# Which pairs of the output projection use seven products, and which use an adding transfer

## The chip, the cores and the metric

The kernel runs on one core of one Trainium2 chip. The metric is the time of one execution on the device, in microseconds; lower is better. A run gives the median of several executions. One more execution is recorded by the hardware profiler, and everything said of single instructions comes from that one.

A core has five engines, each with its own instruction queue, which it works through in order: TensorE (PE; its weight loads are shown as PEld), VectorE (DVE), ScalarE (ACT), GpSimd (POOL) and SyncE (SP). Transfers are started by an engine's queue and carried out by 16 DMA engines that all queues share.

## What is computed

The reference is one layer of a streaming encoder for 256 tokens of 2048 features: a SwiGLU block, a mixer of two recurrent branches, cross-attention over 256 memory tokens, a second SwiGLU block and a norm. Cut to what matters here:

```python
x = x + 0.5 * swiglu(rms_norm(x, ffn1_norm), ffn1_w_up, ffn1_w_down)
h = rms_norm(x, mix_norm)
...
merged = g[:, :, 0, :] * (y_a @ w_branch_a) + g[:, :, 1, :] * (y_b @ w_branch_b)
x = x + merged @ w_out
x = x + cross_attention(rms_norm(x, xattn_norm), rms_norm(mem, mem_norm),
                        xattn_wq, xattn_wkv, xattn_wo)
x = x + 0.5 * swiglu(rms_norm(x, ffn2_norm), ffn2_w_up, ffn2_w_down)
return rms_norm(x, final_norm)
```

The change is in `merged @ w_out`, a product of 256x2048 by 2048x2048. It is called the output projection here.

## The kernel before

**Pieces.** All weights come from memory in pieces of 128 partitions by 2048 float32, 1 MB each, in one planned order for the whole kernel (`plan`). `weights` takes the next piece and keeps up to two prepared ahead of the product that uses them. There are three `raw` buffers for what a transfer brings, three `h` and three `l` buffers for what is made of it.

**High and low halves.** TensorE multiplies in a format with a shortened mantissa. So each operand is split into a high half (ScalarE copies it into the short format, `h`) and a low half (VectorE subtracts, `l = raw - h`; `split`, lines 153 and 154). A product of two operands is three matmuls: high by high and low by high (line 698), high by low (line 700). In `three`, all matmuls of line 698 of a piece come first, then those of line 700, so the low halves of the weights are wanted last.

**Adding transfers.** For some pieces the low half isn't made by VectorE. `begin_added` loads the piece, ScalarE writes `l = -high` (line 289), and a transfer started by GpSimd adds the piece to it on the way in (line 290). That costs a second transfer of the same megabyte, and it is begun one piece earlier in the plan than the piece itself, holding a raw and an l buffer from then on. The high half is then copied at the piece's own turn (line 298).

**The output projection.** Its 2048 output columns are done in two groups of 1024. Each group takes eight pieces, one for each pair of K tiles (2 x 128 rows of `w_out`), so a pair is 256 rows by 1024 columns. With 256 tokens that is a product of 2x2 blocks by 2x2 blocks (token tile by K tile, K tile by half of the columns). A pair is of one of two kinds, set by a letter in `PAIRED`:

- mixed (`m`, or `M` with an adding transfer): eight block products, 24 matmuls of 128x512. Its low half is one VectorE operation of 2048 columns (`m`) or the adding transfer (`M`).
- fast (`f`): seven block products after Strassen's scheme in Winograd's form, 21 matmuls. It needs sums and differences of the weights' blocks (`td`, lines 334, 336 and 338 on VectorE), and these have to be split as well (`th`, `tl`).

Both kinds add into the same seven banks of PSUM (numbers 0 to 6 in `PRODUCTS`). Banks 0, 4 and 5 are used by fast pairs alone. So when the last fast pair of a group is done, `add_residual` with `final` false adds those three to the residual x (one ScalarE copy and six VectorE operations, lines 681 to 685). Behind the last pair of the group, with `final` true, it adds the other four (line 688).

The other operand, the merged activations, is prepared by `Pairs.add` in a turn: eight transposes on TensorE (line 550) and copies and splits on ScalarE and VectorE, for two pairs at a time. For a fast pair it makes four sums (line 630) and splits 512 columns, for a mixed one a difference (line 639) and 256 columns.

**What comes before and after.** The branch projection (`w_branch_a`, `w_branch_b`, lines 393, 394 and 399) precedes; its 16 pieces make the merged activations. After it comes the Q projection of the attention (lines 367 and 370), whose operand is the normed x. That operand, too, is made in turns, `normed`: transposes of x (line 550), scaled copies on ScalarE (line 446), low halves on VectorE (line 448). Each turn makes two of the 16 operands. The first half of x is complete after group 0. Its four turns are held in the list `late`, and `behind_out` lets one of them go behind chosen pairs of group 1. The Q projection begins with products over operands 0 to 7, the ones of these four turns.

**Two other streams** share the queues here. `make_ahead` forms sums of the last block's weights ahead of time: a load into `prep`, four VectorE operations (line 227) and a store (line 228), the load and the store in GpSimd's queue. SP's queue carries all loads of pieces, in plan order. Within an engine the order is laid down when the program is built, mostly that of the text, but an instruction whose operands are expected later can be put behind others that are ready.

Of the kernel before, what the change touches and what calls it, by code (L numbers as in the profile page):

```python
# [46 lines left out]
KINDS = {"m": "mixed", "M": "mixed", "f": "fast", "a": "fast"}  # L47


PAIRED = {"out": "m0 f1 M2 f3 m4 f5 M6 m7"}  # L50


def kinds(name):
    return [e[0] for e in PAIRED[name].split()]

# [38 lines left out]
def block_kernel(ctx: ExitStack, tc: tile.TileContext, xT, xin, memT, vec, gfin, bgate, lruw, wu1, wd1, win, wv,  # L94
# [306 lines left out]
    def flush(late, n=KT):  # L401
        while late and n:
            late.pop(0)()
            n -= 1
# [897 lines left out]
    xs3, sq3 = Operands(), TokenSquares()  # L1302

    def behind_out(g, p):
        if not g or p in (1, 3, 5, 6):
            flush(late, 1)

    for g in range(2):
        pair_products("out", g, pairs_m, add_residual, behind_out)
        for c in (2 * g, 2 * g + 1):  # L1310
            if c == 2:
                root_ready(xt[c])
            sq3.add(c)
            late += [lambda c=c, y=y: normed(xs3, c, "xattn_norm", [y]) for y in range(2)]
# [265 lines left out]
```

## Time and profile before

| what | value |
|---|---|
| median of 3 runs | 2405.73 us (2405.52 to 2405.76) |
| the profiled execution's own time | 2406.76 us |
| its span, first to last instruction | 2405.0 us |
| TensorE clock granted | 0.999 |
| busy: PE, DVE, ACT, POOL | 100%, 85%, 65%, 5% of the span |
| DMA | 640.03 MB, mean 266 GB/s |
| output projection, first to last matmul | 1429.9 to 1515.9 us |
| transfers of `w_out` | 16 loads, 4 adding transfers |

The profile lists busy times by engine, groups of instructions by line, what an idle engine waited for, and the chain of work that ended last, followed back from the end. `acc<-h,ops` means that an instruction writes the tile `acc` and reads `h` and `ops`. In a timeline a row has the start, the duration, the engine, the line and the operation; `xN` are N instructions merged into one row, and a bracket at the end gives the idle time before it and what ended that. Matmuls overlap in the pipeline, so the time that one costs in a row of many is the distance between starts and not its duration.

### The profile page before, as it was taken

What the parts mean: (1) busy time and instruction counts of PE and PEld (TensorE: products, weight loads), DVE (VectorE), ACT (ScalarE), POOL (GpSimd) and SP (SyncE); (2) the same over time, 40 slices, a digit from 0 to 9 for tenths busy, and PEclk for the clock granted to TensorE, in tenths of its full rate; (3) what the DMA queues carried; (4) which work ended last, traced back from release to release, by engine and by line L of the source; (5) the groups of instructions that cost most, each with busy time, mean ns of one, the idle gap of its engine ahead of it and who ended that gap; (6) DMA issues with size and microseconds to landing.
All of it is one profiled execution on the core that took longest, in us unless ns stands there. A gap on an engine that the chain in (4) does not pass through costs nothing.

```text
span 2405.0 us, 31008 instructions
## 1 busy us (share of the span) xinstructions
PE 2393.3 (100%) x12053; PEld 1991.5 (83%) x12053; DVE 2054.2 (85%) x2335; ACT 1560.6 (65%) x1594; POOL 120.1 (5%) x174
## 2 busy tenths in 40 slices
PE   9999999999999999999999999999999999999998
PEld 7888888888888888888888888888888888888887
DVE  7679999999999866778678788765799999999995
ACT  6756777777777654454576456655676677777774
POOL 0000000000000000000000000000000000000000
PEclk9999999999999999999999999999999999999999
DMA  8876889999999757767678768764687899999993
GB/s 301 309 254 223 268 266 266 273 274 278 276 276 276 266 216 291 265 243 289 258 276 334 281 243 262 294 223 162 215 321 299 317 276 276 274 274 273 274 272 129
DMA packets 98739, 640.03 MB, mean 266 GB/s; under 512 B 10976, under 2 KB 11488, under 8 KB 32928
## 3 DMA queue, kind: packets, MB, share of 16 engines
q1 hardware_dynamic: 74160, 493.61, 54.8%
q0 software_dynamic: 24288, 144.19, 24.5%
q8 instruction: 94, 1.54, 0.2%
q14 instruction: 53, 0.43, 0.0%
q10 hardware_dynamic: 144, 0.26, 0.0%
HBM read 601.18 MB, written 36.83 MB: 265 GB/s over the span
## 4 chain that ended last, share of the span: by engine, by line
PE 97%; DVE 2%; DMA 1%; ACT 0%; issue 0%; SPq 0%; ACTq 0%; DVEq 0%
PE acc L698 38%; PE acc L700 19%; PE acc L367 11%; PE acc L393 7%; PE acc L394 7%; PE acc L399 7%; PE acc L370 6%; PE acc L738 1%; PE acc L550 1%; DVE tl L154 1%; DVE l L154 0%; PE acc L1342 0%; PE acc L1088 0%; DMA raw<-t 0%; PE acc L1367 0%
## 5 line engine op out<-in xcount | busy, mean ns | idle before, releaser
L153 ACT ACTIVATE h<-raw 128x2048 fp32r<-128x2048 f32 (+3 forms) x420 | 683.2, 1640 | 412.6 <-PE acc L394 135.0
L154 DVE TENSOR_TENSOR l<-raw,h 128x2048 fp32r<-128x2048 f32 (+2 forms) x365 | 751.6, 2060 | 227.4 <-ACT h L153 224.9
L698 PE MATMUL acc<-h,xh 128*128 128x512 f32 x1221 | 474.6, 391 | 0.6 <-ACT h L153 0.5
L698 PE MATMUL acc<-h,xl 128*128 128x512 f32 x1221 | 473.1, 390 | 0.0
L153 ACT ACTIVATE h<-td 128x1024 fp32r<-128x1024 f32 x287 | 301.0, 1055 | 172.3 <-DVE td L334 53.7
L154 DVE TENSOR_TENSOR tl<-td,h 128x1024 fp32r<-128x1024 f32 x287 | 348.9, 1220 | 13.7 <-ACT h L153 11.8
L698 PE MATMUL acc<-h,hidop 128*128 128x512 f32 x1408 | 351.4, 391 | 0.0
L698 PEld LDWEIGHTS acc<-h,hidop 128*128 128x128 f32 x1408 | 262.7, 188 | 53.8
L698 PEld LDWEIGHTS acc<-h,xh 128*128 128x128 f32 x1221 | 229.1, 188 | 54.6 <-ACT h L153 5.8
L698 PEld LDWEIGHTS acc<-h,xl 128*128 128x128 f32 x1221 | 229.3, 188 | 46.7
L393 PE MATMUL acc<-h,ops 128*128 128x512 f32 x576 | 226.1, 393 | 0.0
L394 PE MATMUL acc<-h,ops 128*128 128x512 f32 x576 | 224.4, 390 | 0.0
L367 PE MATMUL acc<-ops,h 128*128 128x512 f32 x896 | 217.7, 393 | 0.0
L700 PE MATMUL acc<-tl,xh 128*128 128x512 f32 x660 | 193.0, 394 | 0.3 <-DVE tl L154 0.3
L367 PEld LDWEIGHTS acc<-ops,h 128*128 128x128 f32 x896 | 164.1, 188 | 32.6
L700 PE MATMUL acc<-l,hidop 128*128 128x512 f32 x704 | 190.7, 389 | 0.0
L334 DVE TENSOR_TENSOR td<-raw 128x1024 f32<-128x1024 f32 x146 | 178.0, 1219 | 3.5 <-DMA raw<-wout 2.3
L700 PE MATMUL acc<-l,xh 128*128 128x512 f32 x561 | 156.7, 390 | 0.0
L700 PEld LDWEIGHTS acc<-l,hidop 128*128 128x128 f32 x704 | 132.1, 188 | 27.8
L700 PEld LDWEIGHTS acc<-tl,xh 128*128 128x128 f32 x660 | 120.7, 188 | 33.8 <-DVE tl L154 10.1
L399 PE MATMUL acc<-l,ops 128*128 128x512 f32 x576 | 142.3, 389 | 0.0
L399 PEld LDWEIGHTS acc<-l,ops 128*128 128x128 f32 x576 | 108.1, 188 | 22.4
(270 smaller groups left out, 3014.4 us busy)
## 6 DMA issues: line engine op xcount, KB each, us to landing
raw<-wu SPq DMA_DIRECT2D x151, 1024.0 KB, 6.9
raw<-wd SPq DMA_DIRECT2D x88, 1024.0 KB, 7.3
l<-wu POOLq DMA_DIRECT2D x59, 768.0 KB, 8.7
raw<-win SPq DMA_DIRECT2D x40, 1024.0 KB, 4.9
raw<-wg SPq DMA_DIRECT2D x32, 1024.0 KB, 5.4
prep<-wu POOLq DMA_DIRECT2D x25, 1024.0 KB, 7.1
t<-prep POOLq DMA_DIRECT2D x25, 1024.0 KB, 4.6
raw<-t SPq DMA_DIRECT2D x25, 1024.0 KB, 6.5
```

Of the source, the lines that this page charges most:

```text
L153: done["high"] = act.activation(h, raw, ACT.Copy).ins
L154: done["low"] = dve.tensor_tensor(out=l, in0=raw, in1=h.bitcast(F32), op=ALU.subtract).ins
L334: dve.tensor_tensor(out=two[0], in0=raw[:, None, :512].broadcast_to([P, 2, 512]), in1=two[1], op=ALU.subtract)
L367: pe.matmul(acc, h[:, k * P:(k + 1) * P], xs[k], start=k == 0, stop=False)
L370: done["product"] = pe.matmul(acc[:, :T], l[:, k * P:(k + 1) * P], xs[k][:, :T], start=False, stop=k == KT - 1).ins
L393: pe.matmul(accs[t], x[:, t * P:][:, :P], h[j], start=first and j == 0, stop=False)
L394: pe.matmul(accs[t], x[:, T + t * P:][:, :P], h[j], start=False, stop=False)
L399: done["product"] = pe.matmul(accs[t], x[:, t * P:][:, :P], l[j], start=False, stop=last and j == 3).ins
L550: pe.transpose(acc[:, z * T + t * P:][:, :P], tile[:, t * 512 + (2 * y + z) * P:][:, :P], ident)
L698: pe.matmul(acc, a, b, start=start, stop=False)
L700: done["product"] = pe.matmul(acc, ah, bl, start=False, stop=stop).ins
L738: pe.transpose(acc[:, z * T + t * P:][:, :P], hid[t][:, (2 * y + z) * P:][:, :P], ident)
```

## The change

```diff
-PAIRED = {"out": "m0 f1 M2 f3 m4 f5 M6 m7"}
+PAIRED = {"out": "M0 f1 M2 f3 m4 f5 f6 m7"}
...
     def behind_out(g, p):
-        if not g or p in (1, 3, 5, 6):
+        if not g or p in (1, 3, 6, 7):
             flush(late, 1)
```

In both groups pair 6 becomes a fast pair, so that four of eight pairs use seven products where three did. Pair 0 takes an adding transfer; pair 6, which had one, no longer does. The last fast pair of a group is now pair 6 and not pair 5, so the partial eviction moves behind pair 6. In group 1 the four turns of x go behind pairs 1, 3, 6 and 7 instead of 1, 3, 5 and 6.

## The prediction

> **What bounds the kernel.** I read the page's shares first, then the chain of work that ended last, then the chain in order of time around the output projection, then VectorE's and the queues' timelines there.
>
> ```profile
> span 2405.0 us, 31008 instructions
> PE 2393.3 (100%) x12053; PEld 1991.5 (83%) x12053; DVE 2054.2 (85%) x2335; ACT 1560.6 (65%) x1594; POOL 120.1 (5%) x174
> PE 97%; DVE 2%; DMA 1%; ACT 0%; issue 0%; SPq 0%; ACTq 0%; DVEq 0%
> ```
>
> TensorE is busy the whole span and makes up 97% of the chain. A matmul taken away anywhere shortens the end, unless its successor then waits. VectorE at 85% is the only engine near it. The chain through the stage (start, length, matmuls):
>
> ```profile
> 1430.05 3.63 PE acc L698 x16
> 1433.68 1.82 PE acc L700 x8
> ...
> 1456.96 3.17 PE acc L698 x14
> 1460.14 1.59 PE acc L700 x7
> 1461.72 3.63 PE acc L698 x16
> ...
> 1467.16 3.63 PE acc L698 x16
> ...
> 1510.09 0.44 PE acc L550 x4
> ...
> 1514.20 1.81 PE acc L700 x8
> 1516.02 1.81 PE acc L367 x8
> ```
>
> Each pair is 16+8 matmuls (mixed) or 14+7 (fast), with line 700 taking the low halves of the weights. Pair 6 of group 0 runs from 1461.72 to 1467.16, 5.44 us for 24: one matmul per 0.2267 us. (The mean durations in the page's groups are of overlapping matmuls and would overstate the gain.) Pair 5 (fast) takes 4.76 us for 21. No gap stands between pairs, so the stage is TensorE's alone. How near VectorE is (PE, PEld, DVE, ACT, POOL busy per group of columns):
>
> ```profile
> 1429.90:1472.44 42.54, 42.54 (x192) 35.08 (x191) 38.63 (x43) 26.32 (x23) 2.32 (x3) 1.00 0.88 275
> 1472.44:1515.86 43.42, 43.42 (x201) 35.91 (x200) 36.89 (x41) 30.30 (x34) 3.04 (x5) 1.00 0.86 284
> ```
>
> VectorE is busy for 91% of group 0 and 85% of group 1: this change spends that reserve.
>
> **Pair 6 by seven products.** It removes three matmuls per group: 2 x 3 x 0.2267 = 1.36 us, all on the path. The Trainium skill (TensorE: Matmul & The Clock Gate, "Wait — 56ns, not 53.3ns?") has warm 512-column matmuls start every 215.7 ns, by which this term would be 1.29 us. The rows above have 226.7 ns, and the measurement decides.
>
> Where pair 6 gave VectorE nothing (its low half came by an adding transfer), it now takes what fast pair 5 takes:
>
> ```profile
> 1450.29 1.22 DVE L334 TENSOR_TENSOR td<-raw 128x1024 f32<-128x1024 f32 x1
> ...
> 1452.15 1.75 DVE L154 TENSOR_TENSOR l<-raw,h 128x1536 fp32r<-128x1536 f32 x1
> ...
> 1454.42 2.44 DVE L154 TENSOR_TENSOR tl<-td,h 128x1024 fp32r<-128x1024 f32 x2
> 1456.77 2.86 DVE L227 TENSOR_TENSOR prep<-prep 128x512 f32<-128x512 f32 x4
> 1460.36 2.29 DVE L154 TENSOR_TENSOR l<-raw,h 128x2048 fp32r<-128x2048 f32 x1 [0.72 <-ACT h L153]
> ...
> 1466.79 0.69 DVE L682 TENSOR_TENSOR ev<-acc,ev 128x512 f32<-128x512 f32 x1
> ```
>
> From 1450.29 to 1456.77, 6.48 us in all. Pair 0's plain split (2.29 us, as in the 1460.36 row) goes in exchange. Its operand, too, becomes a fast pair's: in the turn of the last merged columns, behind pair 0 of group 0, four small operations and a split of 512 columns take the place of one and a split of 256.
>
> ```profile
> 1394.49 1.02 DVE L630 TENSOR_TENSOR xs<-xs 128x128 f32<-128x128 f32 x4
> 1397.26 0.69 DVE L154 TENSOR_TENSOR xd<-xs,xd 128x512 fp32r<-128x512 f32 x1 [0.24 <-ACT xd L153]
> 1415.87 0.42 DVE L639 TENSOR_TENSOR xs<-xs 128x256 f32<-128x256 f32 x1
> 1416.77 0.42 DVE L154 TENSOR_TENSOR xd<-xs,xd 128x256 fp32r<-128x256 f32 x1 [0.48 <-ACT xd L153]
> ```
>
> That is 1.71 for 0.84, 0.87 us more, in group 0 alone. Its window then asks VectorE for 38.63 + 6.48 + 0.87 - 2.29 (the next group's pair 0 is split inside it) = 43.7 us against 42.54 - 0.68 = 41.9 us of TensorE. Group 1 asks 36.89 + 6.48 = 43.4 against 42.7. What doesn't fit slips past the window's end, as far as TensorE's slack allows, so order decides. ScalarE is far from this (26.32 of 42.54).
>
> In group 0 pair 5 is followed by line 227 (traced after pair 5's split, so ahead of pair 6's), done by about 1459.6, or up to 0.9 later with the larger operand. Pair 6's preparation then ends 6.48 us later, between 1466.1 and 1467.0. Pair 6 starts at 1461.72 and wants its last low half after 14 + 5 matmuls, at 1466.03. That is 0.1 to 1.0 us late, and less if matmuls of pair 7 are put in between; I take 0.4, since VectorE's idle gaps before that (one of 0.72 us in the 1460.36 row) close.
> ```profile
> 1451.62 1.06 ACT L153 ACTIVATE h<-td 128x1024 fp32r<-128x1024 f32 x1
> ...
> 1503.60 2.29 DVE L154 TENSOR_TENSOR l<-raw,h 128x2048 fp32r<-128x2048 f32 x1 [4.46 <-ACT h L153]
> ```
>
> ScalarE's two splits of the sums (1.06 each) must wait for pair 5's h buffer (three exist), free 14 matmuls into pair 5, at 1460.14; the sums are wanted from matmul 7 of pair 6, at 1463.1: room enough. In group 1 VectorE idles 4.46 us ahead of pair 7's split, so pair 6 fits there.
>
> The partial eviction (six VectorE operations like the 1466.79 row, 4.1 us at most) moves from behind pair 5 to behind pair 6. Its banks are wanted by pair 0 of the next group, one pair later: 5.44 us of pair 7 cover it where 10.88 did. Only the first three of the six free banks: even behind pair 7's split they are through 2.29 + 3 x 0.69 = 4.4 us after pair 6. I take 0; uncovered it would be that 4.4.
>
> **Adding transfers for pairs 0.** Their number stays two per group; pair 0's replaces pair 6's. Pair 0 now takes a raw, an l buffer and a place in SP's and POOL's queues one piece before the last piece of the branch projection.
>
> ```profile
> raw<-wab SPq DMA_DIRECT2D x16, 1024.0 KB, 5.0
> ...
> 1404.50 0.33 SPq L307 DMA_DIRECT2D raw<-wout  x1
> 1411.11 1.92 ACT L153 ACTIVATE h<-raw 128x2048 fp32r<-128x2048 f32 x1 [3.52 <-PE acc L394]
> 1413.06 2.29 DVE L154 TENSOR_TENSOR l<-raw,h 128x2048 fp32r<-128x2048 f32 x1 [1.16 <-ACT h L153]
> 1420.67 2.29 DVE L154 TENSOR_TENSOR l<-raw,h 128x2048 fp32r<-128x2048 f32 x1
> 1426.74 0.53 POOL L228 DMA_DIRECT2D t<-prep  x1 [18.55 <-DVE prep L227]
> 1424.65 1.92 ACT L289 ACTIVATE l<-raw 128x2048 fp32r<-128x2048 f32 x1 [0.27 <-PE acc L399]
> L290 POOL DMA_DIRECT2D l<-wout x4: 856/878/888, 1427.3 to 1491.1; - x4
> ...
> DMA to landing us min/median/max: 9.1/10.1/10.9
> ```
>
> The last projection piece gets pair 0's place in SP's queue (1404.50), lands 5.0 us later and is wanted by ScalarE at 1411.11: covered by 1.6 us, and its product only starts at about 1424.6 (24 x 0.2267 before 1430.05). Its VectorE split leaves 1413.06, since pair 0 took the l buffer, and takes the place that pair 0's own split leaves at 1420.67. Pair 0's transfer (last row: the four of line 290) can be issued at about 1415.0 (it takes the l buffer of the 1413.06 row, then ScalarE's 1.92 of the 1424.65 row), ahead of line 228's store, which waits until 1426.74 anyway; it lands by 1425.9 and is wanted at 1433.68. In group 1: buffer free at 1456.96, landed by 1469.8, wanted at 1475.5 (3.63 into that pair, which starts 4.76 + 5.44 after 1461.72). Cover 7.8 and 5.7 us: 0. Without that cover each would cost what it is late.
>
> **Turns behind other pieces.** In group 1 the four turns of x (lines 550, 446, 448) go behind pairs 1, 3, 6, 7 instead of 1, 3, 5, 6. The last one used to have pair 7's 5.44 us after it. Now line 367's first product of Q follows, and its seventh and eighth matmuls read what this turn makes.
>
> ```profile
> 1509.93 0.60 PE L550 MATMUL acc<-vt,x 128*128 128x128 f32 x4
> 1510.57 0.84 ACT L446 ACTIVATE ops<-acc,vt 128x256 fp32r<-128x256 f32 x2 [0.29 <-PE acc L550]
> 1487.04 0.87 DVE L448 SCALAR_TENSOR_TENSOR ops<-acc,vt,ops 128x256 fp32r<-128x256 f32 x2
> 1513.46 2.28 DVE L154 TENSOR_TENSOR l<-raw,h 128x2048 fp32r<-128x2048 f32 x1
> 1515.66 1.88 DVE L688 TENSOR_TENSOR x<-acc,x 128x512 f32<-128x512 f32 x3
> ```
>
> Pair 7 ends at 1516.02 - 1.36 = 1514.66. The turn's matmuls cost 0.44 us wherever they stand. The Q product starts at 1515.1 and reaches its seventh matmul 6 x 0.2267 later, at 1516.46. ScalarE is done 0.64 + 0.84 after 1514.66, at 1516.1. VectorE is then in the three operations of line 688 (1.88, from pair 7's end) until 1516.5, and hands over the operands at 1516.95 and 1517.4: TensorE waits 0.5 to 0.7 us. Lower end 0, if TensorE's order puts other matmuls of Q in between (the low halves and the second product's first six are ready). Upper end 2.8, if a weight split of 2.28, which here stood just ahead of line 688, stands ahead of the turn too. I take 0.4, near the row of line 688, since those operations become ready first.
>
> **Sum.** -1.36 + 0.4 + 0.4 = -0.56 us. The profiled execution took 2406.76 us (span 2405.0 and 1.76 around it), 1.03 above the median; it would come to 2406.2, and the median 2405.73 to **2405.2**. About 0.2%, 4.8 us, is what a measurement of this kernel can tell from no change; this is 0.02%.
>
> **Rivals.**
> A, the forecast: 2404.6 to 2405.8, chance 0.45.
> B, every wait is filled by other matmuls: -1.36, or up to 0.5 more if the lighter start of group 0 helps: 2403.9 to 2404.6. For: no pair of the stage waits in the chain above. Against: VectorE is asked for more than TensorE. 0.25.
> C, the Q product waits for the turn behind a weight split, 2.8 us: -1.36 + 0.4 + 2.8 = +1.8, 2407.6, slower than before. It decides if line 154 stands between pair 7's end and line 448. For: the 1513.46 row. Against: there it fills idle time of VectorE, which after the move is gone. 0.15, from 2406 on by how much of it other matmuls fill.
> D, VectorE's backlog holds pair 6: if a split (2.2) or line 227 (2.86) is ahead of the preparation's last part, each group waits that long: -1.36 + 4.4 to 5.7, 2408.8 to 2410.1. Bound: if all VectorE idle of both groups (42.54 - 38.63 + 43.42 - 36.89 = 10.4) remains beside 87.1 us of work, the stage takes 97.5 for 86.0, 2417. Against: 4.46 us of that idle lies right where group 1 needs it. 0.12.
> E, pair 0's adding transfer is slow: at twice 10.9 us it lands 3.1 us late in group 0 and 5.2 in group 1, -1.36 + 8.3 = +6.9, 2412.6. Against: four such transfers landed within 9.1 to 10.9 us under a VectorE that was 85 to 91% busy. 0.03. The Trainium skill (SBUF — State Buffer, "SBUF: two separate sides") warns of just this: descriptors of a GpSimd-issued transfer can't be written while VectorE holds the shared port, 620 ns becoming 3100. The same page has tensor_tensor outside the mode that does it, and the four landings agree.
>
> That the change does less than it says is hardly possible: one string sets plan, operands and products alike.
>
> **Numbers.** Range 2404.0 to 2407.5: A, B and most of C; D, E and the ends left out come to about 0.2. Slower by over 0.2%: E and a quarter of D, 0.06. Faster by over 0.2%: nothing gives 4.8 us; 0.01. Same: 0.93.
>
> **What would show it.** 12047 matmuls for 12053; 180 plus turns per group. Stage from 1430.05 to the first line 367 matmul: between 84.6 and 85.7 us for 85.97. Right before pair 6's end, line 154's tl<-td on VectorE ends within 1 us of its reader in group 0. Behind pair 7 of group 1, line 367 pauses after six matmuls, with line 448 as releaser. The forecast is wrong if the stage is longer than 86, or if another stage moves by over 1 us.

## The result and the profile after

The change made the kernel slower: median 2413.3 us (2412.05 to 2415.75, 7 runs) against 2405.73 (7 runs by then, 2404.64 to 2408.42), a ratio of 1.0031 with a 95% interval of 1.0021 to 1.0040. The forecast of 2405.2 and its range, up to 2407.5, are both missed. The profiled execution of the changed kernel took 2412.34 us (span 2410.6), 5.6 more than that of the kernel before.

The page of the kernel after, its span, busy times and shares of the chain:

```profile
span 2410.6 us, 31006 instructions
PE 2394.0 (99%) x12047; PEld 1990.8 (83%) x12047; DVE 2062.5 (86%) x2348; ACT 1563.6 (65%) x1598; POOL 120.4 (5%) x174
PE 95%; DVE 2%; DMA 1%; ACT 1%; issue 1%; SPq 0%; ACTq 0%; DVEq 0%
```

The six matmuls are gone (12047 for 12053), but TensorE is no longer busy throughout. Where it stands idle is read from the windows of the two groups of columns and of the Q projection up to the first attention matmul (line 1342); the columns are length, PE, PEld, DVE, ACT and POOL busy with instruction counts, granted clock, DMA share and GB/s. Kernel after:

```profile
1428.96:1470.70 41.74, 41.74 (x190) 34.54 (x188) 41.74 (x50) 25.06 (x23) 2.04 (x3) 1.00 0.74 218
1470.70:1518.66 47.96, 43.78 (x197) 34.95 (x196) 41.74 (x43) 30.51 (x33) 3.04 (x5) 1.00 0.80 271
1518.66:1545.91 27.25, 25.10 (x147) 21.34 (x146) 19.81 (x32) 19.29 (x33) 0.00 (x0) 1.00 0.71 272
```

The same windows of the kernel before; its first group stands in the prediction (42.54):

```profile
1472.44:1515.86 43.42, 43.42 (x201) 35.91 (x200) 36.89 (x41) 30.30 (x34) 3.04 (x5) 1.00 0.86 284
1515.86:1539.92 24.06, 24.06 (x145) 21.31 (x144) 17.40 (x26) 17.04 (x31) 0.00 (x0) 1.00 0.72 275
```

Group 0 is 0.80 us shorter, a little more than its three matmuls, and TensorE never waits in it. Group 1 is 4.54 us longer, and the Q projection 3.19 us longer. Together that is +6.9 us. (The execution after entered the stage 0.93 us earlier, 1428.96 against 1429.89, so its span shows less.) The two places, in TensorE's timeline of the kernel after; the bracket is the idle time before the row:

```profile
1475.68 0.61 PE L700 MATMUL acc<-l,xd 128*128 128x512 f32 x2
1477.78 1.19 PE L698 MATMUL acc<-h,ops 128*128 128x512 f32 x4 [1.48 <-ACT h L153]
...
1480.10 1.20 PE L698 MATMUL acc<-h,xd 128*128 128x512 f32 x4 [0.66 <-ACT h L153]
...
1482.67 0.73 PE L700 MATMUL acc<-tl,xd 128*128 128x512 f32 x2 [0.69 <-DVE tl L154]
...
1485.44 0.74 PE L698 MATMUL acc<-h,xd 128*128 128x512 f32 x2 [1.35 <-ACT h L153]
...
1492.18 1.07 PE L698 MATMUL acc<-h,ops 128*128 128x512 f32 x4
...
1518.66 2.03 PE L367 MATMUL acc<-ops,h 128*128 128x512 f32 x6
1522.85 0.96 PE L367 MATMUL acc<-ops,h 128*128 128x512 f32 x2 [2.15 <-DVE ops L448]
```

The first place is pair 1 of group 1, with some of pair 2 woven into it: four waits, 4.2 us. Pairs 1 and 2 with a turn should take 4.76 + 5.44 + 0.44 = 10.6 us; they take 16.0, from 1476.14 (the first row and two starts) to 1492.18. (The waits in brackets are counted from the modelled ends of matmuls, so the distances between starts show more.) The second place is the seventh matmul of Q. It should start 6 x 0.2267 after 1518.66, at 1520.0, and starts 2.8 us later.

What the first place waits for is read in the queues, SP's first, of the kernel after:

```profile
1449.57 0.33 SPq L288 DMA_DIRECT2D raw<-wout  x1
1454.75 0.33 SPq L307 DMA_DIRECT2D raw<-wout  x1
1461.10 0.33 SPq L288 DMA_DIRECT2D raw<-wout  x1
1464.20 2.86 SPq L327 DMA_DIRECT2D raw<-wout  x2
...
1458.85 0.89 POOL L290 DMA_DIRECT2D l<-wout  x1 [29.30 <-DVE tl L154]
1463.78 0.56 POOL L228 DMA_DIRECT2D t<-prep  x1 [4.05 <-DVE prep L227]
...
1460.35 0.68 DVE L338 TENSOR_TENSOR td<-raw,td 128x512 f32<-128x512 f32 x1
...
1462.27 1.91 ACT L298 ACTIVATE h<-raw 128x2048 fp32r<-128x2048 f32 x1
...
1476.18 1.23 DVE L334 TENSOR_TENSOR td<-raw 128x1024 f32<-128x1024 f32 x1 [4.07 <-DMA raw<-wout]
```

There are three raw buffers. Pair 0 of group 1 takes one at 1449.57 and gives it back only when its high half is copied (line 298), at 1464.18: 14.6 us. Pair 1's load takes that buffer. Pair 6, now fast, holds another until its last difference is made (line 338, until 1461.03), and pair 2's load, which stands first in the queue, takes that one. So SP begins no load between 1454.75 and 1461.10. Then pair 0's adding transfer (1458.85), pair 2's load (1461.10), the store of line 228 (1463.78) and the loads of pairs 1 and 3 (from 1464.20) come on top of one another. Pair 1's load takes 12.0 us, to 1476.18. Before, it left and landed like this:

```profile
1462.68 4.54 SPq L327 DMA_DIRECT2D raw<-wout  x2
...
1470.99 1.23 DVE L334 TENSOR_TENSOR td<-raw 128x1024 f32<-128x1024 f32 x1 [0.52 <-DMA raw<-wout]
```

8.3 us. Counted from the first matmul of the stage the load now leaves 2.4 us later (35.2 us into it, not 32.8) and is 3.7 us slower on the way. The DMA share tells the same (the column before the last, then GB/s). Before:

```profile
1440.00:1460.00 20.00, 20.00 (x90) 16.48 (x89) 18.93 (x20) 13.89 (x10) 0.89 (x1) 1.00 0.78 240
1460.00:1475.00 15.00, 15.00 (x68) 12.43 (x67) 12.13 (x14) 8.39 (x8) 1.43 (x2) 1.00 0.99 347
```

After:

```profile
1440.00:1460.00 20.00, 20.00 (x90) 16.58 (x89) 20.00 (x22) 13.29 (x13) 0.89 (x1) 1.00 0.55 201
1460.00:1475.00 15.00, 15.00 (x67) 12.40 (x67) 12.11 (x16) 6.62 (x5) 1.19 (x2) 1.00 0.99 301
```

In the 20 us in which the engines have room (0.55), the loads can't start; in the next 15 the engines are full and bring less.

The second place, in the chain of waits of the kernel after, in order of time:

```profile
1508.95 2.30 DVE l L154
1511.27 8.27 DMA raw<-wq
1519.64 1.91 ACT h L153
1521.55 0.74 ACT ops L446 x2
1522.31 0.49 DVE ops L448
1522.85 0.96 PE acc L367 x2
```

The turn's copies (line 446) stand on ScalarE's queue behind the copy of a piece of Q (line 153), which waits for a load that left at 1511.27 and lands at 1519.6. So the Q product waits for a late load, through ScalarE's queue. Nothing of VectorE's stands in front of line 448 itself, but the load could leave only when a split on VectorE (line 154, the first row) gave up its raw buffer.

**Theories.** *Buffers and transfers* (mine, after the result): pair 0's adding transfer in group 1 holds a raw buffer, the loads bunch up, pair 1 and later a piece of Q come late. *VectorE* (rival D of the prediction): the four operations of a fast pair 6 and the sums of line 227 push its splits back. *Turn* (rival C): most of the loss is the turn's new place, whatever the loads do. *Slow adding transfer* (rival E).

### The profile page after: what moved, and what is told of

Same layout as the page of the kernel before. It is cut to its first block, busy times and chain, and to the rows that moved or that the text cites. A ratio compares the mean times of both kernels' runs of the same rounds, so it can differ in the third digit from the quotient of the medians.

```text
span 2410.6 us, 31006 instructions
## 1 busy us (share of the span) xinstructions
PE 2394.0 (99%) x12047; PEld 1990.8 (83%) x12047; DVE 2062.5 (86%) x2348; ACT 1563.6 (65%) x1598; POOL 120.4 (5%) x174
## 4 chain that ended last, share of the span: by engine, by line
PE 95%; DVE 2%; DMA 1%; ACT 1%; issue 1%; SPq 0%; ACTq 0%; DVEq 0%
PE acc L698 36%; PE acc L700 18%; PE acc L367 11%; PE acc L393 7%; PE acc L394 7%; PE acc L399 7%; PE acc L370 6%; PE acc L738 1%; DMA raw<-wout 1%; DVE l L154 1%; PE acc L550 1%; ACT h L153 0%; DVE tl L154 0%; DMA raw<-wq 0%; PE acc L1342 0%
## 5 line engine op out<-in xcount | busy, mean ns | idle before, releaser
L154 DVE TENSOR_TENSOR tl<-td,h 128x1024 fp32r<-128x1024 f32 x291 | 353.5, 1220 | 13.7 <-ACT h L153 11.9
```

Source lines behind the costliest of these rows:

```text
L154: done["low"] = dve.tensor_tensor(out=l, in0=raw, in1=h.bitcast(F32), op=ALU.subtract).ins
```

## The experiments

All are edits of the kernel after unless said. "Stage" is the time from the first matmul of the output projection to the first of Q (85.97 before, 89.70 after), which doesn't depend on when an execution reaches it. Ratios are to the kernel before, timed on the same chip (2405.46 to 2405.73 us).

### The change in parts

**The turns put back, all else kept.**

```diff
-        if not g or p in (1, 3, 6, 7):
+        if not g or p in (1, 3, 5, 6):
```

> The changed kernel with the turns of x behind pairs 1, 3, 5, 6 of group 1, as before the change. In the changed kernel TensorE waits in two places: in pair 1 of group 1 (4.2 us) and at the first Q product (2.2 us, some 3 with what follows). If the turn's new place is the cause of the second wait: that wait is gone, pair 1's stays, and the time is 2.2 to 3.2 us below the changed kernel's, about 2410.5. If the second wait comes from late loads and not from the place: it stays in some form, within 1 us of 2413.3.

2410.12 us, 1.0019 (1.0010 to 1.0028). The stage stays at 89.68 and Q to attention falls from 27.25 to 24.41. The waits of TensorE that are left (total, times, longest) are those of pair 1:

```profile
PE acc L698 <- ACT h L153: 3.3, 3, 1.3
PE acc L700 <- DVE tl L154: 0.7, 1, 0.7
```

About 3 of the 7.6 us come by way of the turn.

**The turns alone, with the pairs as before.**

```diff
-PAIRED = {"out": "M0 f1 M2 f3 m4 f5 f6 m7"}
+PAIRED = {"out": "m0 f1 M2 f3 m4 f5 M6 m7"}
```

> The kernel before with the turns alone moved (behind 1, 3, 6, 7). If the place alone costs the wait at the first Q product: 1 to 3 us over the kernel before, 2406.7 to 2408.7. If the wait needs the late load of a Q piece, which ScalarE's queue has ahead of the turn's copies: no more than the 0.4 to 0.7 us of the prediction, 2405.7 to 2406.4.

2406.82 us, 1.0004 (0.9995 to 1.0013); stage 85.78, first Q matmul to attention 24.69 (24.06 before). The median lies just inside the first branch, 1 to 3 us, but its interval begins below no change. In the trace, stage and Q stretch together are 0.44 us longer than before, and TensorE waits 0.2 us at the Q product. That is about what the prediction took for the place. So *Turn* falls as the main cause: the place becomes dear when the loads of Q are late.

**Pair 0 with a plain split, all else kept.**

```diff
-PAIRED = {"out": "M0 f1 M2 f3 m4 f5 f6 m7"}
+PAIRED = {"out": "m0 f1 M2 f3 m4 f5 f6 m7"}
```

> The changed kernel with pair 0 plain: pair 6 fast, no adding transfer for pair 0. If the raw buffer that pair 0's adding transfer holds makes pair 1's load late in group 1: that wait of 4.2 us goes, 2408 to 2410. If VectorE's extra work for pair 6 delays it: VectorE has another 2.29 us per group, so the wait stays or grows, 2413 to 2418.

2406.71 us, 1.0003 (0.9994 to 1.0012); stage 86.81. It is faster than either branch had it. Without pair 0's adding transfers 6.6 of the 7.6 us are gone, though VectorE has more to split. What is left is 1.5 us on line 153 and 0.4 on line 154 in group 1, which eats the six matmuls.

**Only pair 0's adding transfer, without the fourth fast pair**; turns as before.

```diff
+PAIRED = {"out": "M0 f1 M2 f3 m4 f5 m6 m7"}
+        if not g or p in (1, 3, 5, 6):
```

> The kernel before with the adding transfer moved from pair 6 to pair 0, pair 6 plain, three fast pairs, turns as before. No matmul less. If the held raw buffer is the cause: pair 1 of group 1 waits here too, 2 to 5 us over the kernel before, 2407.7 to 2410.7. If VectorE's extra work for the fourth fast pair is the cause: nothing waits, 2405 to 2406.5.

2408.45 us, 1.0011 (1.0002 to 1.0019); stage 87.94. Pair 1's load and its landing:

```profile
1462.60 0.94 SPq L327 DMA_DIRECT2D raw<-wout  x2
...
1474.02 1.23 DVE L334 TENSOR_TENSOR td<-raw 128x1024 f32<-128x1024 f32 x1 [7.65 <-DMA raw<-wout]
```

11.4 us on the way, and 2.8 us of loss, with no fourth fast pair and no moved turn. The adding transfer does harm by itself. The load left 33.1 us into the stage, hardly later than before the change (32.8): it lost its time on the way, not in waiting for a buffer.

**Pair 0 adds in group 0 only.**

```diff
-"M": "added", "f": "fast"}[k]))
+"M": "added", "f": "fast"}["m" if g and not p else k]))
```

> The changed kernel with pair 0's adding transfer in group 0 alone; in group 1 pair 0 is plain. If the buffer held by pair 0 of group 1 is what makes pair 1 of group 1 late: as with pair 0 plain in both groups, 2406 to 2408. If the shift begins in group 0 (loads behind its transfer come later from there on): 2410 to 2413.5.

2406.76 us, 1.0004 (0.9995 to 1.0013); stage 86.23. Leaving out this one transfer in group 1 takes back 6.5 of the 7.6 us, as much as leaving out both: the harm is done at the change of group. Pair 1's load and its first reader:

```profile
1466.09 6.15 SPq L327 DMA_DIRECT2D raw<-wout  x2
...
1473.55 1.21 DVE L334 TENSOR_TENSOR td<-raw 128x1024 f32<-128x1024 f32 x1
```

The load leaves even later than in the kernel after, 37.8 us into the stage for 35.2, but takes 5.7 us for 12.0 and has landed when VectorE comes to it. Nor is a buffer held for less time here: pair 0, plain, keeps its raw buffer for 17.8 us, until its split on VectorE. So what the adding transfer costs is the other loads' time on the way.

### Buffers, transfers or VectorE

**Without the sums of line 227 and the store of line 228 in the middle of this stage**; the kernel does that piece later, its load (line 222) at the end of the stage, its store behind it.

```diff
-    parts.enter_context(scope(wide=3, prep=1))
+    parts.enter_context(scope(wide=3))
```

> The changed kernel without the sums made ahead in this stage: the last one of line 227 (2.86 us of VectorE, a load and a store of 1 MB) moves to the Q projection's stage. Still three raw buffers. If VectorE's backlog in group 0 or the store's share of the DMA engines makes pair 1 of group 1 late: its wait of 4.2 us shrinks, 2408.5 to 2410.5. If it is the raw buffers: no more than 1 us from the changed kernel's 2413.3.

2407.78 us, 1.0010 (1.0001 to 1.0019); stage 86.76. Pair 1's load leaves 35.0 us into the stage (35.2 in the kernel after), but lands 9.4 us later and not 12.0. So raw buffers alone, which this edit leaves at three, don't explain the 12 us. Either the store's megabyte or VectorE's 2.86 us does the rest; the last two runs of this part try to tell these apart. The three sums that stand between the parts of pair 6 in the kernel after don't hold up its raw buffer: pair 2's load, which takes it, leaves 32.4 us into the stage without them and 32.1 with them.

**A fourth raw buffer**, in the room of `prep`, so that the run above is its control.

```diff
-    parts.enter_context(scope(wide=3, prep=1))
+    parts.enter_context(scope(wide=3, raw1=1))
```

> As the run before, and the freed room is a fourth raw buffer for this stage (every fourth load goes to it). If loads wait for raw buffers that the adding transfers hold: pair 1's load is issued earlier, its wait of 4.2 us is gone, and the late Q piece in front of the turn's copies on ScalarE too: 2405 to 2408. If pair 1 is late for another reason (its landing takes 12.0 us for 8.2, DMA engines shared): within 1 us of the run before.

2404.81 us, 0.9996 (0.9987 to 1.0005); stage 84.40. Pair 1's load, its landing, and a window over the rest of the stage, which ends at 1512.53, and a little more (PE and DVE busy are the second and the fourth column):

```profile
1460.49 3.20 SPq L327 DMA_DIRECT2D raw<-wout  x2
...
1470.02 1.23 DVE L334 TENSOR_TENSOR td<-raw 128x1024 f32<-128x1024 f32 x1 [2.27 <-DMA raw<-wout]
...
1470.00:1515.00 45.00, 45.00 (x205) 36.60 (x204) 44.47 (x48) 31.12 (x35) 2.72 (x5) 1.00 0.80 277
```

The load leaves 32.4 us into the stage, as early as before, and TensorE waits nowhere, with VectorE busy for 44.47 of 45 us. The stage is 1.57 us shorter than before: the six matmuls' 1.36 at last. Against its control the buffer is worth 3.0 us. A VectorE that is 99% busy delays nothing here, which speaks against *VectorE* as far as pair 6's own operations go. It doesn't end that theory, for the sums of line 227 are not in this stretch.

**The same two edits on the kernel before.**

> The kernel before with a fourth raw buffer in place of the sums made ahead in this stage: the control for the run of the changed kernel with that buffer (2404.8). TensorE waits nowhere in this stage before the change, so the buffer has nothing to give: 2405.2 to 2406.2, and the 0.9 us between is the six matmuls. If it comes to 2404.8 or less, the buffer or the move of the sums gave it and the six matmuls nothing.

2406.04 us, 1.0002 (0.9992 to 1.0011); stage 85.96. The buffer gives nothing where no load was late. Against this run the one above has a stage shorter by 1.56 us, with the same buffers: that is the six matmuls.

**The store cut to 16 columns.** The rest of the piece is copied, without the sums, by a transfer of its own when the piece is loaded; VectorE's work stays, but the kernel leaves most of these sums out of what it stores.

```diff
-        nc.gpsimd.dma_start(t, src)
+        nc.gpsimd.dma_start(t, src); made_ahead or nc.gpsimd.dma_start(to[:, 16:], src[:, 16:])
...
-        nc.gpsimd.dma_start(to, t)
+        nc.gpsimd.dma_start(*(v if made_ahead else v[:, :16] for v in (to, t)))
```

> The changed kernel with every engine's order unchanged; only the last store of line 228 (1 MB, at 1463.78 in the changed kernel) moves 16 of 2048 columns. The other columns of that tile are copied, without the sums, much earlier, so one piece of the last block's weights is wrong. Theory: pair 1's load of group 1 is late because it shares full DMA engines with the loads of pairs 2 and 3, pair 0's adding transfer and this store. Then it lands 2 to 3 us earlier and the time falls by 2 to 4 us, to 2409.5 to 2411.5. Rival, VectorE's backlog: nothing changes on VectorE, 2412.5 to 2414.

2414.62 us, 1.0035 (1.0022 to 1.0047); stage 86.75. Pair 1's load and its landing:

```profile
1468.66 2.80 SPq L327 DMA_DIRECT2D raw<-wout  x2
...
1477.63 1.23 DVE L334 TENSOR_TENSOR td<-raw 128x1024 f32<-128x1024 f32 x1 [1.12 <-DMA raw<-wout]
```

9.0 us for 12.0, leaving 35.3 us into the stage as ever, and the stage is 2.95 shorter. The store's megabyte was in the loads' way. The median doesn't follow, and misses the forecast. In the profiled execution (2415.12 us) the stage begins 4.4 us later than in that of the kernel after, at 1433.36 for 1428.96. Of this, 3.4 us are lost in the first 235 us, where the edit changes nothing. The Q stretch is 1.4 us longer (28.65): the wait at the Q product remains, 2.5 us, and the clock fell behind it (last section). The other executions have no trace.

**VectorE's last four sums of line 227 cut to 16 columns**, the store whole; the sums of the other columns are left out.

```diff
-                dve.tensor_tensor(out=b[o], in0=b[x], in1=b[y], op=ALU.subtract)
+                dve.tensor_tensor(out=(q := lambda v: v[:, :512 if made_ahead else 16])(b[o]), in0=q(b[x]), in1=q(b[y]), op=ALU.subtract)
```

> The changed kernel with the last four operations of line 227 on 16 columns for 512 (2.86 us of VectorE in group 0 become about 0.5); the store stays whole, with wrong sums. If VectorE's backlog makes the loads late (pair 6's preparation holds the buffer that pair 2's load of group 1 waits for): 2408.5 to 2411. If the transfers alone do: within 1 us of 2413.3.

2415.85 us, 1.0043 (1.0030 to 1.0055); stage 91.82. Pair 1's load still takes 11.9 us (1464.41 to 1476.28). Taking about 2 us from VectorE (four operations of 0.68 us became 0.16 to 0.17) does not bring the load in sooner. So of the landing's 12.0 us the store accounts for about 3: 9.4 with neither, 9.0 with the sums alone, 11.9 with the store alone. For the time of the whole kernel it is a weak test, and outside both forecasts: shorter operations also changed the order that is laid down when the program is built, the stage grew, and the clock fell in it after a wait of 3.9 us (0.72 in the window from 1484 to 1490).

### Where an adding transfer may stand

**Four fast pairs, pair 0 plain, old turns**, and **the same with pair 4 as the second one with an adding transfer**:

```diff
+PAIRED = {"out": "m0 f1 M2 f3 m4 f5 f6 m7"}
...
+PAIRED = {"out": "m0 f1 M2 f3 M4 f5 f6 m7"}
```

> Four fast pairs, pair 0 plain, turns as before the change (behind 1, 3, 5, 6). If the turn's place costs 1 to 3 us by itself: 2404 to 2405.7, the three matmuls of each group at last seen in part. If with pair 0 plain the turn's place costs nothing: 2406.7 as with pair 0 plain and the new place. If VectorE (another 2.29 us per group) is the bound: 2406 to 2408, with TensorE's waits in group 1 as there.

> Four fast pairs with adding transfers for pairs 2 and 4, pair 0 plain, turns as before the change: the same work on every engine as with pairs 0 and 2, held buffers elsewhere. If the trouble is that pair 0's transfer falls on the change of group, where pair 6's preparation and the store crowd VectorE and the DMA engines: 2404.5 to 2406.5. If any second adding transfer beside a fourth fast pair starves the loads: 2408.5 to 2411.

2406.34 us, 1.0003 (0.9994 to 1.0011), stage 86.81; and 2406.49 us, 1.0004 (0.9995 to 1.0013), stage 86.86. The second does the same matmuls, splits and adding transfers as the kernel after with its turns put back (2410.12), with one of the latter in the middle of a group and not at its start: 3.6 us less, so the place decides. Neither gains: TensorE still waits for 1.7 and 1.4 us at the start of group 1. In the first run VectorE has no gap up to there (PE and DVE busy are the second and the fourth column):

```profile
1430.00:1470.00 40.00, 40.00 (x182) 33.07 (x181) 40.00 (x48) 25.55 (x23) 1.42 (x2) 1.00 0.68 222
```

Pair 1's load took 5.7 us and landed at 1472.9; VectorE came to it at 1474.71. So with pair 0 plain VectorE comes last, as the third branch had it, and *VectorE* explains what is left there. In the second run the load itself comes last, by 0.2 us. The small difference between these two causes isn't settled.

## Why the prediction was wrong, point by point

- **Six matmuls: right.** Group 0 shows it at once (41.74 for 42.54), the run with the fourth buffer for the whole stage (-1.57 against before, -1.56 against its own control, for -1.36).
- **VectorE late for pair 6 in group 0, +0.4: it cost nothing.** VectorE was as full as worked out, 41.74 of 41.74 us, and TensorE did not wait. But pair 6's raw buffer went at 1461.03 only, and no term asked who waited for that: pair 1's load left 2.4 us later than before. With four fast pairs and pair 0 plain, TensorE waits for 1.3 to 1.9 us in group 1, about what the matmuls save or more.
- **The partial eviction behind pair 6, 0: right.** Pair 0 of group 1 starts without a wait.
- **Adding transfers for pairs 0, "Cover 7.8 and 5.7 us: 0": this is the step that failed.** What it worked out held. Its buffer free at 1456.96 and ScalarE's 1.92 us make an issue at 1458.9, and it gave the landing as 1469.8 at the latest. Pair 0's transfer in group 1 was issued at 1458.85 and landed after 8.8 us, at 1467.7, ahead of line 700's 1474.3.

```profile
L290 POOL DMA_DIRECT2D l<-wout x1: 887/887/887, 1458.8 to 1458.8; - x1
...
DMA to landing us min/median/max: 8.8/8.8/8.8
```

What failed is "Without that cover each would cost what it is late": the price was taken to be the transfer's own lateness. It left out what the transfer does to the loads beside it. This transfer, the loads of pairs 2, 1 and 3 and the store are all begun within 8 us, and pair 1's load took 12.0 us for 8.3. Without the transfer in group 1 that load took 5.7 us. The raw buffer, which one would suspect first, isn't the price: without the transfer the load left later still (37.8 us into the stage for 35.2). In group 0 the prediction did follow SP's queue to the displaced load; in group 1 it followed only the transfer itself. The price was 5.4 us in pairs 1 and 2, and the pause at Q, which is gone in the run without the transfer in group 1.

- **Turns behind other pieces, +0.4: right in place, wrong in the blocker and in size.** Line 367 paused after six matmuls with line 448 as releaser, as foretold. But line 448 waited for ScalarE's copies, behind a copy that waited for a load: 2.8 us. Rival C named a VectorE split just ahead of line 448 as the blocker; none stands there, VectorE idled 2.2 us. With loads in time the pause is 0.2 us.
- **The rivals.** B fell: not every wait was filled. D fell as it was put: TensorE waits inside pair 6 in neither group. E came near in amount (2412.6) for another reason: its own transfer wasn't slow, 8.8 us where it asked for 21.8. The Trainium skill's "SBUF — State Buffer", "SBUF: two separate sides", by which VectorE's hold on the shared port would keep back such a transfer's descriptors, doesn't show here: the landing is below the 9.1 to 10.9 us before, with VectorE busier. The prediction had tensor_tensor outside that stall, and VectorE ran tensor_tensor without a gap from the transfer's issue to its landing.
- **The sign for error held:** "wrong if the stage is longer than 86, or if another stage moves by over 1 us"; the stage was 89.7, and the Q stretch moved by 3.2. A loss of over 0.2% had been given a chance of 0.06; it came to 0.31%.

**Open.** The store's share in pair 1's landing, about 3 us, rests on a run that moves a transfer as well, and on one in which the order changed; that the two agree with the run without either is what speaks for it. How the rest divides between the adding transfer's own time on the DMA engines and the loads that start together with it isn't shown. The median after lies 1 us above the profiled execution; the last section has a likely reason. The fourth buffer's 0.9 us under the median before is within what the measurement can't tell; in the stage's own time it is seen.

## What to carry to other kernels

The price of a transfer is not only what it is late itself. In this case the transfers that ran beside it came late by it, and an adding transfer took twice a load's time on the DMA engines. So where an edit lets several transfers start at nearly the same time, add up what they all take of the engines. When a load comes late, read apart when it left and how long it was on the way: a buffer shows in the first, other transfers in the second, and between two of these runs they moved in opposite directions. A wait that is cheap at its new place stays cheap only while nothing ahead of it on its engine's queue waits for memory.

## What the runs showed of the hardware

**An adding transfer took twice as much of the DMA engines as a load; a store did not.** The DMA queues have packets, MB and the share of 16 engines; q0 is GpSimd's, q1 SP's. In the kernel before, from 1405 to 1425 us, the one transfer of GpSimd is a store of line 228:

```profile
q0 software_dynamic: 144, 1.05, 13.6%
```

In the run without sums and store, from 1454.5 to 1476.5 us, GpSimd has adding transfers alone and SP loads alone:

```profile
q1 hardware_dynamic: 576, 4.19, 47.4%
q0 software_dynamic: 183, 1.37, 34.7%
```

The store is 13.6% of 20 us, 2.7 us for 1.05 MB, or 2.6 us per MB. The loads are 10.4 us for 4.19 MB, 2.5 per MB. The adding transfers are 7.6 us for 1.37 MB, 5.6 per MB. So of all that started together at the change of group, pair 0's adding transfer was the dearest.

**A short wait can cost twice.** In the run with the small store TensorE waits 2.5 us at the Q product, in the one with the small sums 1.9. Then, in windows of 2 us (granted clock third from the end), the small store first:

```profile
1524.00:1526.00 2.00, 1.38 (x4) 1.12 (x5) 1.92 (x4) 0.46 (x3) 0.00 (x0) 0.52 0.99 418
1526.00:1528.00 2.00, 2.00 (x13) 2.00 (x12) 2.00 (x3) 1.97 (x5) 0.00 (x0) 0.62 1.00 423
```

The small sums:

```profile
1526.00:1528.00 2.00, 2.00 (x11) 1.96 (x10) 2.00 (x4) 1.73 (x4) 0.00 (x0) 0.52 1.00 422
1528.00:1530.00 2.00, 2.00 (x11) 1.92 (x11) 2.00 (x2) 1.99 (x7) 0.00 (x0) 0.63 0.97 402
```

From the end of that wait to the first attention matmul it takes 24.1 and 24.6 us, and 23.1 in the kernel after, for the same matmuls: 1.1 and 1.55 us are lost on top of the wait. The profiled execution of the kernel after, with 2.15 us of wait at the same matmul, kept 1.00, so the length of the wait alone doesn't decide. But four of its seven runs have a mean clock of 0.998, not 0.999, and they are the ones at or above the median (2413.3 to 2415.75); 0.1% of this kernel is 2.4 us. Of all profiled executions here the two with the drop have 0.998, the others 0.999. That such a drop makes those four runs longer is likely and not shown, since they have no trace. The Trainium skill ("TensorE: Matmul & The Clock Gate", "What's actually happening") has half the clock pulses passed after an idle window of about 3.4 us that runs freely. The 0.52 agrees with its half speed. A wait of 2.5 us is shorter than its window, and here the clock fell all the same.
